# Where the gathered-row steps stand in VectorE's queue: pinned by an estimate of when their row lands, with a finer estimate of each instruction

## Chip, cores and metric

One core of a Trainium2 chip. The metric is the device time of one launch in microseconds; the time before is 3278.47 us, the median of three runs (3274.97 to 3279.72).

## What is computed

One residual block on 1024 tokens of width 1024, in f32. The last of its three parts is PEER: each token picks 16 of 16384 single-neuron experts for each of 8 heads.

```
x = x + hybrid_mixer(rmsnorm(x))         # gated DeltaNet (4 heads) | RG-LRU, one projection in, one out
x = x + cross_attention(rmsnorm(x), rmsnorm(mem))
x = x + peer_ffn(rmsnorm(x))
out = rmsnorm(x)

def peer_ffn(h):
    q = (t @ wq)                         # 8 heads x 2 halves of 128
    s1, i1 = top_k(q1 @ subkeys1, 16);  s2, i2 = top_k(q2 @ subkeys2, 16)
    best, pos = top_k(s1[:, None] + s2[None, :], 16)
    idx = i1[pos // 16] * 128 + i2[pos % 16];  gate = softmax(best)
    act = gelu(einsum('phkd,pd->phk', u_tab[idx], t)) * gate
    return einsum('phk,phkd->pd', act, v_tab[idx])
```

## The kernel before

**Stages.** The mixer works through four chunks of 256 tokens (tiles qkv, cy, lxf, W, gd, go); attention and the choice of experts follow it in units of 128, 128, 256, 256 and 256 tokens (X, hT, sc, s, i, cand, best, pos, e). For tokens 256 to 767 the experts are done densely: a gate stage turns the chosen indices into a gate matrix (one-hot rows oh from iot and keys, scaled on ScalarE into ohg, multiplied on TensorE into gd, copied into stage and written out), and a dense stage then runs 128 blocks of 128 experts (`hidden` and `out`: dh, dg, dah, dal, po; 48 matmuls of 512 columns per block). For the other four blocks of 128 tokens each expert row is gathered: GpSimd issues one indirect DMA of 128 rows of 4 KB (`fetch`, L1134), and VectorE does one **row step** on it (`step`): 512 steps take the dot product with u (rb, hdot), 512 add a row of v scaled by ga. So there are 1024 row steps, of which every one is a scalar_tensor_tensor over 128x1024; six row buffers (NROW) turn over, five gathers run ahead.

**What sets the order.** The kernel is traced as Python; streams (`together`) hand over pieces by an estimate of the time. Class `Engine` keeps it: every traced instruction goes through `f`, and `spend` adds a fixed part and a rate per element to the engine's clock `at` and remembers when each tile is ready (`known`). `Paced.tick` does so for TensorE, and whenever its clock has advanced by `pace` it traces a row step (before the dense stage only if VectorE's clock is less than SLACK ahead and the oldest row is estimated to have landed, `late_row`). `moved` estimates when a transfer lands. In the dense stage (`pe.real` off) the pace counts TensorE's work alone.

The framework then schedules the trace: each engine takes its instructions by trace order as they become ready in the framework's own reckoning, so an instruction whose input is not ready is overtaken by later ones. A row step is exempt: `tc.keep_in_program_order` puts it behind everything that VectorE was given before it in the trace. On the chip each engine runs its own queue strictly in that final order.

All VectorE and ScalarE instructions carry L82 (the helper's call), matmuls L106, transposes L111, the gathers L1134; so rows are told apart by tiles.

Of the kernel before, what the change touches and what calls it, by code (L numbers as in the profile page):

```python
# [8 lines left out]
F = mybir.dt.float32  # L9
BF = mybir.dt.bfloat16  # L10
# [3 lines left out]
AF = mybir.ActivationFunctionType  # L14
OP = mybir.AluOpType
# [3 lines left out]
S = 1024  # L19
# [4 lines left out]
TD = 2 * T  # L24
# [11 lines left out]
RANK = (1, 1, 1, 0)  # L36
HOP, SLACK, WAIT = 100.0, 8000.0, 1000.0
SHARE = (6.0, 1.0, 6.0, 1.0)
L_NORM, L_STEP, L_CONV, L_SOFT, L_GATE = 14000.0, 2500.0, 4000.0, 6000.0, 1500.0
PACES = (2800.0, 2800.0, 2800.0, 3500.0)  # L40
PACE_G, PACE_D = 3500.0, 2250.0
FIRST = 0
EARLY = T
UNITS = ((0, 1), (128, 1), (256, 2), (512, 2), (768, 2))
# [5 lines left out]
def block_kernel(ctx: ExitStack, tc: tile.TileContext, a):  # L50
# [21 lines left out]
    class Engine:  # L72

        def __init__(self, engine, fixed, rate):
            self.engine, self.fixed, self.rate = engine, fixed, rate
            self.at = self.total = self.end = 0.0

        def __getattr__(self, op):
            call = getattr(self.engine, op)

            def f(*args, **kw):
                r = call(*args, **kw)  # L82
                aps = [x for x in list(args) + list(kw.values()) if isinstance(x, bass.AP)]
                if op == "dma_start":
                    moved(prod(args[0].shape) * 4)
                else:
                    self.spend(aps)
                return r
            return f

        def spend(self, aps, n=0):
            t0 = max([self.at] + [known(x) for x in aps[1:]])
            ns = self.fixed + self.rate * (n or max(prod(x.shape[1:]) for x in aps))
            self.at = t0 + ns
            self.end = max(self.end, self.at)
            self.total += ns
            wrote(aps[0], self.at + HOP)

    class Paced(Engine):
# [5 lines left out]
        def matmul(self, out, l, r, **kw):  # L105
            self.engine.matmul(out, l, r, **kw)  # L106
            self.rate = 1.67 if r.dtype == F else 0.42
            self.tick([out, l, r])

        def transpose(self, out, i, ident):  # L110
            self.engine.transpose(out, i, ident)  # L111
            self.rate = 0.43
            self.tick([out, i])
# [10 lines left out]
    sp = Engine(nc.sync, 0.0, 0.0)  # L124
    act, dve = Engine(nc.scalar, 200.0, 0.72), Engine(nc.vector, 68.0, 1.04)

# [978 lines left out]

    todo, fetched = [], []
    blocks = {}
# [31 lines left out]
    def late_row():  # L1139
        return bool(fetched) and fetched[0][4] > max(dve.at, pe.at) + WAIT  # L1140

    def step():
        while todo and len(fetched) < NROW - 1:
            fetch()
        if not fetched:
            return False
        row, ph, k, t, _ = fetched.pop(0)
        B = blocks[row]
        if ph == "u":
            if k == 0:  # L1150
                dve.scalar_tensor_tensor(B["h"], B["h"], B["rs"], B["w"], op0=OP.mult, op1=OP.mult)
                B["hd"] = gat.tile([128, 128], F, name="hdot", bufs=1)
            tc.keep_in_program_order(
                dve.scalar_tensor_tensor(t, t, 1.0, B["h"], op0=OP.mult, op1=OP.mult,
                                         accum_out=B["hd"][:, k:k + 1]))
            if k == 120:
# [6 lines left out]
        else:  # L1163
            tc.keep_in_program_order(
                dve.scalar_tensor_tensor(B["x"], t, B["a"][:, k:k + 1], B["x"], op0=OP.mult, op1=OP.add))
            if k == 127:
# [98 lines left out]
    with tc.tile_pool(name="dn", bufs=1, side="right") as d2, \  # L1265
            tc.tile_pool(name="dps", bufs=1, space=bass.MemoryType.PSUM) as dps:
        pe.pace, pe.real = PACE_D, False
        dense(dn[0], d2, dps, hT, raws)
# [66 lines left out]
```

## Time and profile before

| | |
|---|---|
| median of three runs | 3278.47 us |
| the profiled execution's own time | 3275.43 us |
| its span | 3273.7 us |
| TensorE (PE) busy | 2987.4 us, 91% |
| VectorE (DVE) busy | 2737.6 us, 84% |
| ScalarE (ACT) busy | 1277.8 us, 39% |
| GpSimd (POOL) busy | 1431.4 us, 44% |
| moved by DMA | 941.66 MB, mean 288 GB/s |

The busy times are sums over the whole span. The stages have different limits, so the sections below read the trace by stretches, which are bounded by events found in VectorE's timeline: the first convolution cy of the second, third and fourth mixer chunk (392, 712, 1055 us), the first one-hot row of the gate stage (1353 us), the first matmul of the dense stage (1790 us), and TensorE's last instruction (3255 us).

### The profile page before, as it was taken

The numbers are of one execution on the slowest core, as the hardware profiler recorded it, in microseconds if no ns is written. First come the engines' busy times: TensorE is split into PE (matmuls) and PEld (weight loads), VectorE is DVE, ScalarE is ACT, GpSimd is POOL, SyncE is SP. The second block draws the span as 40 slices with busy tenths as digits, with TensorE's granted clock in tenths as the row PEclk, the third lists the DMA queues.
The fourth block names the chain that finished last, engine by engine and source line by source line (L and its number), as shares of the span: only waits on it lengthen the run. The fifth ranks groups of instructions, "written<-read, shape, count | busy, mean of one in ns | idle before, by whom it ended". The sixth has DMA issues, their size and how long they took to land.

```text
span 3273.7 us, 46519 instructions
## 1 busy us (share of the span) xinstructions
PE 2987.4 (91%) x16212; PEld 2559.6 (78%) x16212; DVE 2737.6 (84%) x5999; ACT 1277.8 (39%) x2694; POOL 1431.4 (44%) x1046
## 2 busy tenths in 40 slices
PE   6999997699999989898857899999999999999998
PEld 6888887678988878887746677888888878888886
DVE  7634776877787898898999798888999989899998
ACT  6843363236322642376357332222222222222222
POOL 0000233334433344243345375556666655566663
PEclk9999998899999999998968899999999999999999
DMA  5346788688888769888888799999999899999995
GB/s 170 110 143 208 248 281 308 232 285 284 308 292 291 251 223 332 301 281 302 303 289 273 267 329 334 333 340 330 344 333 328 319 334 333 330 341 327 339 331 198
DMA packets 321547, 941.66 MB, mean 288 GB/s; under 512 B 28912, under 2 KB 108832, under 8 KB 319264
## 3 DMA queue, kind: packets, MB, share of 16 engines
q0 software_dynamic: 148048, 538.04, 46.8%
q1 hardware_dynamic: 107216, 367.08, 30.9%
q10 hardware_dynamic: 66048, 33.56, 3.7%
q8 instruction: 128, 2.10, 0.3%
q14 instruction: 107, 0.88, 0.1%
HBM read 894.53 MB, written 44.04 MB: 287 GB/s over the span
## 4 chain that ended last, share of the span: by engine, by line
PE 61%; DVE 20%; DMA 9%; ACT 5%; issue 3%; POOL 1%; SPq 0%; ACTq 0%; DVEq 0%; POOLq 0%
PE dh L106 21%; PE po L106 20%; PE pj L106 15%; DVE rb L82 6%; DMA rb<-in_u,idx 4%; PE gd L106 3%; DVE oh L82 3%; DMA gd<-stage 2%; DMA w<-in_pwq 1%; PE tp L111 1%; PE sc L106 1%; DVE cy L82 1%; ACT ohg L82 1%; DVE i L82 1%; ACT L82 1%
## 5 line engine op out<-in xcount | busy, mean ns | idle before, releaser
L1134 POOL DMA_INDIRECT rb<-in_u,idx x512 | 677.4, 1323 | 1111.9 <-DVE rb L82 497.0
L1134 POOL DMA_INDIRECT rb<-in_v,idx x512 | 745.0, 1455 | 690.3 <-DVE rb L82 478.7
L82 DVE SCALAR_TENSOR_TENSOR rb<-rb 128x1024 f32<-128x1024 f32 x512 | 613.1, 1218 | 90.2 <-DMA rb<-in_u,idx 90.2
L82 DVE SCALAR_TENSOR_TENSOR rb<-rb,ga 128x1024 f32<-128x1024 f32 x512 | 655.0, 1279 | 11.2 <-DMA rb<-in_v,idx 4.9
L106 PE MATMUL pj<-hT,w 128*128 128x256 f32 (+1 forms) x2880 | 590.6, 358 | 16.2 <-DMA w<-in_pwq 11.8
L106 PEld LDWEIGHTS pj<-hT,w 128*128 128x128 f32 x2880 | 491.8, 195 | 73.5 <-DMA w<-in_pwq 13.1
L106 PE MATMUL dh<-hT_h,uh 128*128 128x512 f32 x1024 | 407.1, 398 | 21.4 <-ACT dg L82 20.7
L106 PE MATMUL po<-vh,dah 128*128 128x512 f32 x1024 | 404.8, 395 | 9.7 <-DVE acc L82 8.7
L106 PE MATMUL dh<-hT_l,uh 128*128 128x512 f32 x1024 | 406.2, 397 | 0.0
L106 PE MATMUL dh<-hT_h,ul 128*128 128x512 f32 x1024 | 406.1, 397 | 0.0
L106 PE MATMUL po<-vh,dal 128*128 128x512 f32 x1024 | 405.2, 396 | 0.4 <-DVE dal L82 0.4
L106 PE MATMUL po<-vl,dah 128*128 128x512 f32 x1024 | 405.3, 396 | 0.0
L82 ACT CAST uh<-ur 128x1024 fp32r<-128x1024 f32 x128 | 134.7, 1052 | 561.0 <-PE dh L106 352.8
L106 PE MATMUL gd<-ohg,oh 128*128 128x128 f32 x1024 | 183.7, 332 | 81.4 <-ACT ohg L82 54.5
L106 PEld LDWEIGHTS dh<-hT_h,uh 128*128 128x128 f32 x1024 | 193.2, 189 | 69.3 <-ACT dg L82 21.6
L106 PEld LDWEIGHTS gd<-ohg,oh 128*128 128x128 f32 x1024 | 163.8, 228 | 101.9 <-ACT ohg L82 80.5
L106 PEld LDWEIGHTS po<-vh,dah 128*128 128x128 f32 x1024 | 192.3, 188 | 58.4 <-DVE acc L82 10.0
L106 PEld LDWEIGHTS dh<-hT_h,ul 128*128 128x128 f32 x1024 | 193.0, 189 | 47.0
L106 PEld LDWEIGHTS dh<-hT_l,uh 128*128 128x128 f32 x1024 | 193.2, 189 | 46.4
L106 PEld LDWEIGHTS po<-vl,dah 128*128 128x128 f32 x1024 | 192.3, 188 | 47.2
L106 PEld LDWEIGHTS po<-vh,dal 128*128 128x128 f32 x1024 | 192.3, 188 | 47.1 <-DVE dal L82 0.8
L82 DVE TENSOR_TENSOR ul<-ur,uh 128x1024 fp32r<-128x1024 f32 x128 | 156.0, 1222 | 48.7 <-ACT uh L82 27.6
(339 smaller groups left out, 4757.4 us busy)
## 6 DMA issues: line engine op xcount, KB each, us to landing
ur<-in_ut SPq DMA_DIRECT2D x128, 512.0 KB
vr<-in_v SPq DMA_DIRECT2D x128, 512.0 KB
w<-in_wA SPq DMA_DIRECT2D x80, 512.0 KB
w<-in_pwq SPq DMA_DIRECT2D x80, 512.0 KB
gd<-stage ACTq DMA_DIRECT2D x32, 1024.0 KB
G<-gd SPq DMA_DIRECT2D x16, 2048.0 KB
w<-in_wout SPq DMA_DIRECT2D x40, 512.0 KB
w<-in_wq SPq DMA_DIRECT2D x40, 512.0 KB
```

Of the source, the lines that this page charges most:

```text
L82: r = call(*args, **kw)
L106: self.engine.matmul(out, l, r, **kw)
L111: self.engine.transpose(out, i, ident)
L1134: pool.indirect_dma_start(out=t, out_offset=None, in_=a[ph], in_offset=bass.IndirectOffsetOnAxis(ap=B["idx"][:, k:k + 1], axis=0))
```

## The change

1. A row step is no longer held behind everything traced. `behind` looks through a log of VectorE's traced instructions with their estimated ends, takes the last one that is estimated to be over by the time the row lands plus WAIT (1 us), and ties the step behind that one and behind the step before it (an order alone, no semaphore).
2. The estimate goes by form of instruction: `form` adds a fixed part for an accumulated output, for a per-partition scale on ScalarE, for a table load there, for a scalar_tensor_tensor, a max_index and a match_replace on VectorE; it doubles the scan and halves bf16. The constants of all three engines rise or change (VectorE's fixed part from 68 to 150 ns).
3. The paces change with it: 2800 to 3200 (in the estimate's ns of TensorE), 3500 to 4000, and in the dense stage from a fixed 2250 to DENSE over the steps that are left, so that these are spread over the whole of it.

```diff
-HOP, SLACK, WAIT = 100.0, 8000.0, 1000.0
+HOP, SLACK, WAIT = 130.0, 8000.0, 1000.0
-PACES = (2800.0, 2800.0, 2800.0, 3500.0)
-PACE_G, PACE_D = 3500.0, 2250.0
+PACES = (3200.0, 3200.0, 3200.0, 4000.0)
+PACE_G, DENSE = 4000.0, 1441000.0
+TABLES = {AF.Exp: (0,), AF.Tanh: (0, 1), AF.Gelu_apprx_tanh: (1,), AF.Sqrt: (2,)}
...
-                    self.spend(aps)
+                    self.spend(aps, *self.form(op, args, kw, aps))
+                    self.log.append((r.ins, self.at))
...
+        def form(self, op, args, kw, aps):
+            n = max(prod(x.shape[1:]) for x in aps)
+            more = 0.0
+            if self is act:
+                if isinstance(kw.get("scale"), bass.AP):
+                    more += 130.0
+                if "accum_out" in kw:
+                    more += 200.0
+                tables = TABLES.get(args[2]) if len(args) > 2 else None
+                if tables and self.table not in tables:
+                    self.table = tables[0]
+                    more += 1280.0
+            else:
+                if op == "scalar_tensor_tensor":
+                    more += 60.0
+                if "accum_out" in kw or op in ("max_index", "match_replace"):
+                    more += 80.0
+                if op == "tensor_tensor_scan":
+                    n *= 2
+                elif n > 64 and all(x.dtype == BF for x in aps):
+                    n //= 2
+            return n, more
...
-            self.rate = 1.67 if r.dtype == F else 0.42
+            self.rate = 1.7 if r.dtype == F else 0.46
...
-            self.rate = 0.43
+            self.rate = 0.85
...
-    act, dve = Engine(nc.scalar, 200.0, 0.72), Engine(nc.vector, 68.0, 1.04)
+    act, dve = Engine(nc.scalar, 165.0, 0.83), Engine(nc.vector, 150.0, 1.04)
...
+    def behind(r, land):
+        past = [i for i, t in dve.log[:-1] if t <= land + WAIT][-1:] + steps[-1:]
+        for i in past:
+            tc.add_manual_dep(r.ins, i.name, mybir.DependencyInfo(
+                mybir.DependencyClass.NoSync, mybir.DependencyReason.DATA), reason="rows")
+        steps.append(r.ins)
+        del dve.log[:-200]
...
-        row, ph, k, t, _ = fetched.pop(0)
+        row, ph, k, t, land = fetched.pop(0)
+        stepped[0] += 1
...
-            tc.keep_in_program_order(
-                dve.scalar_tensor_tensor(t, t, 1.0, B["h"], op0=OP.mult, op1=OP.mult,
-                                         accum_out=B["hd"][:, k:k + 1]))
+            behind(dve.scalar_tensor_tensor(t, t, 1.0, B["h"], op0=OP.mult, op1=OP.mult,
+                                            accum_out=B["hd"][:, k:k + 1]), land)
...
-            tc.keep_in_program_order(
-                dve.scalar_tensor_tensor(B["x"], t, B["a"][:, k:k + 1], B["x"], op0=OP.mult, op1=OP.add))
+            behind(dve.scalar_tensor_tensor(B["x"], t, B["a"][:, k:k + 1], B["x"],
+                                            op0=OP.mult, op1=OP.add), land)
...
-        pe.pace, pe.real = PACE_D, False
+        pe.pace, pe.real = DENSE / (2.0 * (S - TD) - stepped[0]), False
```

What the finished programs hold is the same in kind and number, but for one instruction of ScalarE's (a table load); the order differs on every engine before the dense stage. Counted in VectorE's queue, by the stretches named above (bounds by the same instructions in both programs; 32 MAX_INDEX on pos are the choice of experts for two blocks of 128 tokens, its first level is MAX_INDEX on i):

| stretch of VectorE's queue | row steps before, after | MAX_INDEX on pos | MAX_INDEX on i | oh<-oh |
|---|---|---|---|---|
| second chunk (392 to 712 us) | 98, 112 | 16, 16 | 32, 32 | 25, 25 |
| third chunk (712 to 1055 us) | 117, 115 | 0, 32 | 60, 64 | 0, 15 |
| fourth chunk (1055 to 1353 us) | 99, 135 | 32, 32 | 48, 64 | 40, 45 |
| gate stage, first to last one-hot row (1353 to 1790 us) | 127, 116 | 64, 32 | 84, 64 | 40, 20 |
| after it | 583, 546 | 0, 0 | 0, 0 | 40, 40 |

Two places in VectorE's queue show it. First the end of the fourth chunk's recurrence, whose products W (masks wm, levels 5 and 6) TensorE waits for. Before, six steps stand in one run behind the level's W, and the next unit's first-level choice (s, i) follows:

```order
L82 SCALAR_TENSOR_TENSOR n_y<-n_t,n_y 128x2
L82 TENSOR_TENSOR W<-gd,wm_85 128x512
L82 COPY rs_512_11047<-n_y 128x2
L82 TENSOR_TENSOR oh<-oh,ib 128x1024
L82 TENSOR_TENSOR oh<-oh 128x64x8
L82 TENSOR_TENSOR oh<-oh 128x64x4
L82 TENSOR_TENSOR oh<-oh 128x64x2
L82 TENSOR_TENSOR e_384_11079<-oh 128x64
L82 SCALAR_TENSOR_TENSOR rb,hdot<-rb 128x1024 x6
L82 MAX s_0_11125<-sc 128x8
L82 MAX_INDEX i_0_11127<-s_0_11125,sc 128x8
```

The same place in the changed program:

```order
L84 MATCH_REPLACE mr_11708<-best,cand 128x80
L84 SCALAR_TENSOR_TENSOR rb,hdot<-rb 128x1024
L84 TENSOR_TENSOR W<-gd,wm_85 128x512
L84 MAX best<-mr_11708 128x8
L84 SCALAR_TENSOR_TENSOR rb,hdot<-rb 128x1024
L84 MAX_INDEX pos<-best,mr_11708 128x8
L84 SCALAR_TENSOR_TENSOR rb,hdot<-rb 128x1024 x2
L84 MAX best<-cand 128x8
L84 TENSOR_TENSOR W<-gd,wm_86 128x512
L84 MAX_INDEX pos<-best,cand 128x8
L84 MATCH_REPLACE mr_11733<-best,cand 128x80
```

The steps now stand singly between the small instructions of a choice (best, pos) that came in the gate stage before, and up to two of them directly ahead of a W.

Second the dense stage, one pair of expert blocks. Before, nine steps stand from one pair's first ul to the last vl, four or three of them in a run:

```order
L82 TENSOR_TENSOR dal<-dg,dah 128x512
L82 SCALAR_TENSOR_TENSOR rb<-rb,ga 128x1024 x4
L82 TENSOR_TENSOR ul<-ur,uh 128x1024
L82 TENSOR_TENSOR dg<-dg,G 128x512
L82 TENSOR_TENSOR acc<-acc,po_20072 128x512
L82 TENSOR_TENSOR dal<-dg,dah 128x512
L82 SCALAR_TENSOR_TENSOR rb<-rb,ga 128x1024 x3
L82 TENSOR_TENSOR acc<-acc,po_20102 128x512
L82 TENSOR_TENSOR vl<-vr,vh 128x1024
L82 SCALAR_TENSOR_TENSOR rb<-rb,ga 128x1024
```

The like rows of the changed program:

```order
L84 TENSOR_TENSOR dal<-dg,dah 128x512
L84 SCALAR_TENSOR_TENSOR rb<-rb,ga 128x1024 x4
L84 TENSOR_TENSOR ul<-ur,uh 128x1024
L84 TENSOR_TENSOR dg<-dg,G 128x512
L84 TENSOR_TENSOR acc<-acc,po_19170 128x512
L84 SCALAR_TENSOR_TENSOR rb<-rb,ga 128x1024
L84 TENSOR_TENSOR dal<-dg,dah 128x512
L84 SCALAR_TENSOR_TENSOR rb<-rb,ga 128x1024 x2
L84 TENSOR_TENSOR acc<-acc,po_19200 128x512
L84 TENSOR_TENSOR vl<-vr,vh 128x1024 x2
L84 SCALAR_TENSOR_TENSOR rb<-rb,ga 128x1024
```

One of the three steps that followed dal now stands ahead of it, and the second vl is no longer parted from the first by a step. TensorE's queue in the dense stage is the same in both programs.

## Rows read from the trace of the kernel before

**Rows 1.** Busy time by stretch, all engines (stretch, its us, busy us and instructions by engine):

```profile
core 0: us, PE busy (x) PEld busy (x) DVE busy (x) ACT busy (x) POOL busy (x), PEclk, DMA share, GB/s
392.00:712.00 320.00, 266.32 (x1731) 242.50 (x1730) 244.57 (x755) 118.89 (x301) 116.75 (x102) 0.89 0.79 274
...
712.00:1055.00 343.00, 322.98 (x2018) 289.50 (x2018) 269.63 (x708) 131.09 (x328) 134.19 (x117) 0.99 0.84 294
...
1055.00:1353.00 298.00, 272.61 (x1776) 247.76 (x1776) 255.66 (x837) 122.26 (x295) 113.00 (x95) 0.98 0.78 274
...
1353.00:1790.00 437.00, 343.04 (x1944) 305.17 (x1944) 404.88 (x1251) 279.79 (x770) 168.04 (x129) 0.86 0.88 290
...
1738.00:1790.00 52.00, 41.73 (x232) 35.46 (x231) 48.93 (x80) 49.57 (x144) 26.21 (x16) 0.93 0.92 276
...
1857.00:3255.00 1398.00, 1387.99 (x5938) 1114.92 (x5937) 1272.52 (x1511) 397.68 (x505) 859.91 (x560) 1.00 0.90 327
```

**Rows 2.** Waits of PE, 392 to 712 us (who waited for whom: us, times, longest):

```profile
PE tp L111 <- DVE go L82: 11.6, 1, 11.6
...
PE gd L106 <- DVE best L82: 6.5, 3, 4.4
```

**Rows 3.** Groups of DVE instructions, 1055 to 1353 us (busy us, mean ns, idle before):

```profile
L82 DVE SCALAR_TENSOR_TENSOR rb<-rb 128x1024 f32<-128x1024 f32 x58 | 69.5, 1216 | 10.1 <-DMA rb<-in_u,idx 10.1
...
L82 DVE SCALAR_TENSOR_TENSOR rb<-rb,ga 128x1024 f32<-128x1024 f32 x35 | 44.6, 1275 | 0.2
```

**Rows 4.** DMA totals, 1055 to 1353 us (q0: packets, MB, share of 16 engines):

```profile
DMA packets 24616, 81.74 MB, mean 274 GB/s; under 512 B 2604, under 2 KB 5164, under 8 KB 24591
...
q0 software_dynamic: 13383, 48.73, 47.1%
```

**Rows 5.** Waits of PE, 1353 to 1790 us:

```profile
PE gd L106 <- ACT ohg L82: 54.5, 51, 5.3
...
PE gd L106 <- DVE oh L82: 15.5, 5, 6.2
```

**Rows 6.** Groups of DVE instructions, 1353 to 1790 us:

```profile
L82 DVE FIND_INDEX8 i<-s,sc 128x8 uint32<-128x128 f32 x42 | 11.8, 281 | 0.0
...
L82 DVE FIND_INDEX8 i<-s,mr 128x8 uint32<-128x128 f32 x42 | 11.6, 276 | 0.0
...
L82 DVE MATCH_REPLACE8 mr<-s,sc 128x128 f32<-128x128 f32 x42 | 11.4, 272 | 0.0
...
L82 DVE MAX8 s<-sc 128x8 f32<-128x128 f32 x42 | 11.4, 279 | 0.0
...
L82 DVE MAX8 s<-mr 128x8 f32<-128x128 f32 x42 | 11.4, 271 | 0.0
...
L82 DVE FIND_INDEX8 pos<-best,mr 128x8 uint32<-128x80 f32 x32 | 7.4, 231 | 0.0
...
L82 DVE FIND_INDEX8 pos<-best,cand 128x8 uint32<-128x80 f32 x32 | 7.4, 231 | 0.0
...
L82 DVE MAX8 best<-mr 128x8 f32<-128x80 f32 x32 | 7.3, 229 | 0.1
...
L82 DVE MATCH_REPLACE8 mr<-best,cand 128x80 f32<-128x80 f32 x32 | 7.1, 223 | 0.0
...
L82 DVE MAX8 best<-cand 128x8 f32<-128x80 f32 x32 | 7.0, 229 | 0.0
...
L82 DVE TENSOR_TENSOR oh<-oh 128x512 bf16<-128x512 bf16 (+2 forms) x24 | 7.8, 323 | 0.2
...
L82 DVE TENSOR_TENSOR oh<-oh,ib 128x1024 bf16<-128x1024 bf16 x8 | 5.5, 684 | 0.1
...
L82 DVE TENSOR_TENSOR oh<-oh,iota 128x1024 bf16<-128x1024 bf16 x8 | 5.4, 680 | 0.1
```

**Rows 7.** Waits of PE from 1790 us to the end:

```profile
PE dh L106 <- ACT dg L82: 20.7, 2, 17.9
...
PE po L106 <- DVE acc L82: 8.7, 3, 5.2
```

More of the change, by code (lines that the diff above doesn't have):

```diff
@@ L76, in __init__ @@
             self.at = self.total = self.end = 0.0
+            self.table, self.log = None, []
         def __getattr__(self, op):
@@ L86, in f, with spend @@
                 else:
-                    self.spend(aps)
-                return r
-            return f
-        def spend(self, aps, n=0):
+                    self.spend(aps, *self.form(op, args, kw, aps))
+                    self.log.append((r.ins, self.at))
+                return r
+            return f
+        def form(self, op, args, kw, aps):
[20 more added lines that the diff above has]
+            return n, more
+        def spend(self, aps, n=0, more=0.0):
             t0 = max([self.at] + [known(x) for x in aps[1:]])
-            ns = self.fixed + self.rate * (n or max(prod(x.shape[1:]) for x in aps))
+            ns = self.fixed + more + self.rate * (n or max(prod(x.shape[1:]) for x in aps))
             self.at = t0 + ns
@@ L1101, in dense @@
         finish(acc, row3, xs[0][:, NT - 1, :])
-    todo, fetched = [], []
+    todo, fetched, stepped = [], [], [0]
     blocks = {}
@@ L1140, in late_row @@
         return bool(fetched) and fetched[0][4] > max(dve.at, pe.at) + WAIT
+    def behind(r, land):
[5 more added lines that the diff above has]
+        del dve.log[:-200]
+    steps = []
     def step():
```

## The prediction, made before the changed kernel ran

> **What bounds the kernel now.** I read the busy times by stretch first [rows 1]. They show three regimes. From 1857 to 3255 us TensorE is busy for 1387.99 of 1398 us: the dense stage runs at TensorE's own pace, and VectorE, at 1272.52 us, fits beside it. So nothing done for VectorE there can give back more than TensorE's idle time. From 1353 to 1790 us, the gate stage (G), VectorE is busy for 404.88 of 437 us (93%) and TensorE for 343.04: VectorE is the bound, but for the last 52 us, where ScalarE is busy for 49.57. The waits of TensorE agree: 54.5 us for ohg, which waits for oh, and 15.5 us for oh itself [rows 5]. The three mixer chunks before it (A to 712, B to 1055, C to 1353 us) are mixed: TensorE is busy 83%, 94% and 91%, VectorE 76%, 79% and 86%. In A part of what TensorE lacks comes from VectorE's order: 11.6 us for go and 6.5 us for best [rows 2].
>
> **The change part by part.** No instruction of VectorE's is added, so its total work stays; the question is in which stretch it stands, which the counts in the two programs say, and how well it fills the gaps.
>
> *Row steps.* One takes 1216 or 1275 ns in C [rows 3], say 1.25 us. A gets 14 more (+17.5 us of VectorE's time), B two fewer (-2.5), C 36 more (+45), G 11 fewer (-14), the rest 37 fewer (-46). Each takes its gather along: C gets 36 more on GpSimd, which was busy there for 113.00 us with 95 instructions [rows 1], 1.19 us each, so about 156 of some 300 us; that queue holds little else. SyncE's loads for a block of rows stay as many. The pin is an order and no semaphore, so no new wait is issued; what it changes is who stands behind whom. A step whose row is late now holds back VectorE instructions that were traced before it, where it used to hold back only later ones.
>
> *The choice of experts.* With the new estimate the streams hand over in another order. In G 32 of 64 MAX_INDEX on pos, 20 of 84 on i and 20 of 40 oh<-oh go. By the rows of G [rows 6]: half of the five pos and best groups (36.2 us) is 18.1 us, 20/84 of the five i and s groups (57.6 us) is 13.7 us, half of the three oh groups (18.7 us) is 9.4 us; 41 us, and I add nothing for the small rest. The same 32 on pos turn up in B, with 15 oh<-oh and 4 on i (18.1 + 7.0 + 2.7 = 28 us); C gets 16 on i and 5 oh<-oh (11.0 + 2.3 = 13 us).
>
> So VectorE's work becomes: A 244.57 + 17.5 = 262 us, B 269.63 + 28 - 2.5 = 295, C 255.66 + 45 + 13 = 314, G 404.88 - 14 - 41 = 350, and some 46 less of the rest.
>
> *A (320 us).* 262 us of VectorE's work fit easily. At best the two waits of TensorE go (-18), at worst all the added work shows (+17.5). I take -3, since the steps now give way to a choice but also stand ahead of other things.
>
> *B (343 us).* 295 us is 86%, the share at which C runs now, while TensorE, 94% busy, sets the length. From -5 to +28 (all of what is added beyond the steps it loses); I take +5, near what VectorE's 73 idle us can hide.
>
> *C (298 us).* 314 us do not fit into 298. VectorE without any gap gives +16; with the 42 us of idle time that it has now, +58. Transfers bound it as well: 81.74 MB pass now, of which q0, the gathers, 48.73 [rows 4], for 93 steps [rows 3] 0.524 MB each. 135 steps make 70.7 MB, with the 33.0 of the rest 104 MB; at the 327 GB/s of the dense stage [rows 1] that is 317 us, +19. I take +30, which is VectorE at 96%: the single placement is made to fill gaps, but G, where VectorE is the bound, reaches 93% with what lies open to it.
>
> The Trainium skill, DMA: Bandwidth & Descriptors, Specifications, puts the limit of HBM per core at about 358 GB/s; by it the 104 MB would take an estimated 290 us, less than the stretch has now, and transfers would be no bound in C. The dense stage's 327 GB/s is at a DMA share of 0.90 [rows 1], so the trace does not contradict that limit; the sum goes by the row, and by the page it would be the same, since VectorE's own time is the larger of the two.
>
> *G (437 us).* At its present 93%, 350 us of work take 378 us, -59; if TensorE took over at B's 94%, 343.04 us would take 365, -72. If only half of the 70 us that TensorE waits for ohg and oh go, -35: the last 52 us are ScalarE's and cannot shrink. I take -47, midway between -35 and -59.
>
> *Dense stage.* The steps per pair of blocks fall from about nine to about eight and a half. Of TensorE's idle time 20.7 us are a wait for dg, of which one of 17.9 us stays, at the stage's start; 8.7 us are for acc, which steps stand ahead of [rows 7]. From -9 to +3; I take -6. What follows 3255 us stays.
>
> **Sum.** -3 + 5 + 30 - 47 - 6 = -21 us against the profiled execution's 3275.43 us, so 3254. The median of the runs is 3.0 us above that execution, so **3257 us** against 3278.47. If all ends fell on one side the sum would run from -88 (-18 - 5 + 16 - 72 - 9) to +72 (17.5 + 28 + 58 - 35 + 3).
>
> **Rivals.**
>
> *Nothing net (3278 us).* C gives back what G gains, -40 against +40. For it: VectorE's work is the same to the instruction, and from 392 to 1790 us it is busy 1174.7 of 1398 us and gets another 46. Against it: there were 223 us idle to put them in.
>
> *C chokes (slower, 3299 us).* A step that stands ahead of earlier work stops VectorE until its row lands; in C that costs 10.1 us already [rows 3], and gathers come 1.45 times as often there. Then the 42 us of idle time stay, C costs +58 where I have +30, and TensorE, waiting more, is granted less clock: 0.98 in C now, 0.89 in A, where it waits more [rows 1]. Between its two levels of 1.2 and 2.4 GHz that step down costs 272.61 x (0.98 / 0.89 - 1) = 27.6 us of its work; half of it, 14 us, is what I price. 58 - 30 + 14 = 42 more than the forecast's sum: -21 + 42 = +21, with everything else as forecast, 3299. It decides from the point at which C takes over 45 us longer than now. For it: VectorE above 100% of the old length; against it: singly placed steps let the chain through more often than a run of six.
>
> The Trainium skill, Perfetto Trace Analysis, section Matmul Optimizations, says that TensorE scales its power with its use, so that matmuls should run back to back in batches; it speaks against a stretch that VectorE holds up. The trace agrees in kind: G, where TensorE waits most, is granted 0.86, the dense stage 1.00 [rows 1]. By it alone C would lose the whole 28 us.
>
> *All of it overlaps (3209 us).* A -8, B 0, C +16, G -68, dense stage -9: -69. For it: 223 us of idle time and a finer estimate that keeps choices from being piled up in front of go. Against it: C's floors.
>
> *The change not doing what it says:* the log keeps 200 instructions, and a step could find none early enough and be tied to the step before alone. The queues show otherwise (no runs longer than seven); under 2%, and it would look like the second rival.
>
> **How the numbers follow.** What a measurement can tell here is about 0.2%, 6.6 us, so faster is under 3272 and slower above 3285. The forecast (3225 to 3272) gets 0.45; no net change 0.15; C choking 0.25, spread from 3285 to 3325; full overlap 0.15, spread from 3190 to 3225. Faster is 0.45 + 0.15 = 0.60, same 0.15, slower 0.25. Below 3202 lies some 0.07 and above 3306 some 0.10, so the range is 3202 to 3306; the forecast's own is 3225 to 3272.
>
> **What would show it.** Right: in the busy times by stretch, bounded by the same instructions, C at 320 to 340 us with VectorE at 95% or more, G at 375 to 405 us, TensorE's waits for ohg and oh together at 25 to 45 us, the dense stage within 10 us of before with acc below 5 us. Wrong: C not longer (then the gaps took it all, and the third rival stands), C above 345 us with waits of rb for its gather above 25 us and a clock under 0.95 (second), or G hardly shorter (then ScalarE or TensorE bounds it, and the choice was beside it).

## The result: 0.9% slower, by the fourth chunk

The changed kernel takes 3303.75 us (median of 4 runs, 3302.12 to 3312.40), the kernel before 3276.72 us (4 runs, 3273.17 to 3279.72). The ratio is 1.0088, with an interval of 1.0067 to 1.0109. The forecast was 3257 us: the sign is wrong. The time lies inside the range of 3202 to 3306, near where the rival "C chokes" (3299) had put it. The profiled execution of the changed kernel took 3302.98 us, its span is 3301.2 us.

One correction comes first. The bounds that stand ahead for the second, third and fourth chunk (392, 712 and 1055 us) are wrong: I read them off rows of the timeline in which several cy rows are merged. By the first cy row of each chunk they are 356.0, 689.4 and 1029.3 us, so [rows 1] cut each of these stretches 23 to 36 us late. The starts of the gate stage and of the dense stage were right, and the counts of row steps went by instructions, so they stand. From here on A, B, C, G and the dense stage (with what follows it) are cut by the same instructions in every kernel.

The kernel before, busy time by stretch (columns as in [rows 1]):

```profile
356.00:689.40 333.40, 278.29 (x1816) 253.82 (x1815) 246.87 (x762) 125.08 (x317) 117.79 (x104) 0.90 0.78 274
689.40:1029.30 339.90, 319.44 (x2001) 285.95 (x2000) 267.80 (x716) 129.70 (x325) 136.46 (x118) 0.98 0.84 296
1029.30:1353.00 323.70, 298.31 (x1895) 270.24 (x1894) 278.50 (x892) 130.96 (x320) 118.97 (x101) 0.98 0.79 274
1353.00:1789.90 436.90, 342.94 (x1944) 305.07 (x1943) 404.78 (x1251) 279.69 (x770) 167.94 (x129) 0.86 0.88 290
1789.90:3273.70 1483.80, 1439.95 (x6144) 1155.74 (x6144) 1335.28 (x1635) 423.55 (x538) 882.67 (x577) 0.99 0.89 322
```

The changed kernel, the same five stretches (its lines have moved: L84 is the helper of VectorE and ScalarE, L133 the matmuls, L138 the transposes):

```profile
358.80:695.70 336.90, 273.92 (x1824) 250.16 (x1823) 258.97 (x792) 125.53 (x318) 141.73 (x117) 0.91 0.81 293
695.70:1042.80 347.10, 324.07 (x2015) 288.77 (x2014) 292.44 (x910) 138.00 (x337) 137.64 (x116) 0.98 0.82 290
1042.80:1420.70 377.90, 325.88 (x1968) 291.83 (x1966) 326.87 (x1047) 133.03 (x320) 163.65 (x137) 0.92 0.81 292
1420.70:1836.60 415.90, 322.71 (x1847) 290.58 (x1847) 356.81 (x915) 276.05 (x761) 168.50 (x119) 0.85 0.86 283
1836.60:3301.20 1464.60, 1437.39 (x6144) 1154.86 (x6144) 1285.25 (x1596) 419.49 (x535) 773.51 (x538) 0.99 0.87 312
```

Read the second number of each row. The first chunk, which ends at the first row, grew by 2.8 us, A by 3.5, B by 7.2 and C by 54.2; G fell by 21.0 and the dense stage by 19.2. The sum is +27.5, the difference of the two spans. So the whole loss, twice over, is in C. In C VectorE (the third busy time) went from 278.50 to 326.87 us, its share from 86.0% to 86.5%: it took on 48 us of work, and its idle time there did not shrink. TensorE's matmuls there rose from 1895 to 1968, its busy share fell from 92% to 86% and its clock from 0.98 to 0.92.

VectorE's waits in C, before and then after:

```profile
DVE rb L82 <- DMA rb<-in_u,idx: 10.1, 6, 3.3
DVE X L82 <- PE pj L106: 7.5, 6, 2.0
```

```profile
DVE X L84 <- PE pj L133: 19.1, 7, 4.0
DVE rb L84 <- DMA rb<-in_u,idx: 10.2, 13, 1.2
```

The waits for gathered rows of u are the same, 10.1 and 10.2 us; what grew is the wait for TensorE's projections. TensorE in turn waits in C for things that VectorE makes on the recurrence's chain. After the change:

```profile
PE tp L138 <- DVE go L84: 11.1, 1, 11.1
PE gd L133 <- DVE g L84: 6.9, 1, 6.9
PE tp L138 <- ACT oT L84: 5.4, 2, 5.1
PE pj L133 <- ACT lge L84: 4.4, 3, 1.9
```

Of these go had 2.4 us before. In G the forecast had TensorE's two waits on the one-hot rows fall from 70 to between 25 and 45 us. They stayed, 55.0 and 15.3 us against [rows 5]:

```profile
PE gd L133 <- ACT ohg L84: 55.0, 42, 10.4
PE gd L133 <- DVE oh L84: 15.3, 7, 3.9
```

From the dense stage's start TensorE's waits did fall, from [rows 7]:

```profile
PE dh L133 <- ACT dg L84: 12.1, 2, 11.4
PE po L133 <- DVE acc L84: 1.6, 1, 1.6
```

### The profile page after: what moved, and what is told of

The parts are those of the page before. It is cut to its first block, busy times and chain, and to the rows that moved or that the text cites. A ratio compares the mean times of both kernels' runs of the same rounds, so it can differ in the third digit from the quotient of the medians.

```text
span 3301.2 us, 46535 instructions
## 1 busy us (share of the span) xinstructions
PE 2994.6 (91%) x16212; PEld 2567.2 (78%) x16212; DVE 2724.2 (83%) x5999; ACT 1281.2 (39%) x2693; POOL 1392.6 (42%) x1046
## 4 chain that ended last, share of the span: by engine, by line
PE 66%; DVE 16%; DMA 9%; ACT 5%; issue 4%; POOL 1%; SPq 0%; ACTq 0%; DVEq 0%; POOLq 0%
PE dh L133 21%; PE po L133 21%; PE pj L133 17%; DVE rb L84 5%; PE gd L133 3%; DVE oh L84 2%; DMA gd<-stage 2%; PE sc L133 2%; DMA subk<-in_subk 2%; DMA rb<-in_u,idx 1%; PE tp L138 1%; DMA w<-in_wA 1%; ACT ohg L84 1%; DMA w<-in_pwq 1%; ACT L84 1%
## 5 line engine op out<-in xcount | busy, mean ns | idle before, releaser
L1161 POOL DMA_INDIRECT rb<-in_v,idx x512 | 707.2, 1381 | 793.9 <-DVE rb L84 511.7
L84 DVE SCALAR_TENSOR_TENSOR rb<-rb,ga 128x1024 f32<-128x1024 f32 x512 | 655.6, 1280 | 13.4 <-DMA rb<-in_v,idx 8.0
L84 DVE SCALAR_TENSOR_TENSOR rb<-rb 128x1024 f32<-128x1024 f32 x512 | 612.3, 1220 | 21.1 <-DMA rb<-in_u,idx 21.0
L133 PE MATMUL pj<-hT,w 128*128 128x256 f32 (+1 forms) x2880 | 587.6, 358 | 17.5 <-DMA w<-in_pwq 10.5
L133 PEld LDWEIGHTS pj<-hT,w 128*128 128x128 f32 x2880 | 493.6, 194 | 77.1 <-DMA w<-in_pwq 11.5
L133 PE MATMUL dh<-hT_h,uh 128*128 128x512 f32 x1024 | 406.8, 397 | 12.8 <-ACT dg L84 12.1
L133 PE MATMUL dh<-hT_l,uh 128*128 128x512 f32 x1024 | 406.2, 397 | 0.0
L133 PE MATMUL dh<-hT_h,ul 128*128 128x512 f32 x1024 | 406.1, 397 | 0.0
L133 PE MATMUL po<-vh,dah 128*128 128x512 f32 x1024 | 404.0, 394 | 1.6 <-DVE acc L84 1.6
L133 PE MATMUL po<-vl,dah 128*128 128x512 f32 x1024 | 404.9, 395 | 0.0
L133 PE MATMUL po<-vh,dal 128*128 128x512 f32 x1024 | 404.3, 395 | 0.0
L84 ACT CAST uh<-ur 128x1024 fp32r<-128x1024 f32 x128 | 134.6, 1052 | 593.0 <-PE dh L133 339.1
L84 DVE TENSOR_TENSOR ul<-ur,uh 128x1024 fp32r<-128x1024 f32 x128 | 156.6, 1224 | 115.6 <-ACT uh L84 72.5
L133 PE MATMUL gd<-ohg,oh 128*128 128x128 f32 x1024 | 180.6, 333 | 75.6 <-ACT ohg L84 55.0
L133 PEld LDWEIGHTS dh<-hT_h,uh 128*128 128x128 f32 x1024 | 193.0, 188 | 60.8 <-ACT dg L84 13.0
L133 PEld LDWEIGHTS gd<-ohg,oh 128*128 128x128 f32 x1024 | 163.5, 231 | 92.2 <-ACT ohg L84 84.6
L133 PEld LDWEIGHTS po<-vh,dah 128*128 128x128 f32 x1024 | 191.9, 187 | 49.1 <-DVE acc L84 2.1
L133 PEld LDWEIGHTS dh<-hT_h,ul 128*128 128x128 f32 x1024 | 193.0, 188 | 47.0
L133 PEld LDWEIGHTS dh<-hT_l,uh 128*128 128x128 f32 x1024 | 193.1, 189 | 46.5
L133 PEld LDWEIGHTS po<-vl,dah 128*128 128x128 f32 x1024 | 192.1, 188 | 47.3
L133 PEld LDWEIGHTS po<-vh,dal 128*128 128x128 f32 x1024 | 192.1, 188 | 46.1
```

Of the source, the lines that this page charges most:

```text
L1161: pool.indirect_dma_start(out=t, out_offset=None, in_=a[ph], in_offset=bass.IndirectOffsetOnAxis(ap=B["idx"][:, k:k + 1], axis=0))
```

## The experiments

The change has three parts (pin, estimate, paces). The theory that these rows suggest: the pin helps, and the 36 more row steps in C cost more than G and the dense stage return. The rivals: the pin itself hurts, since freer steps stand ahead of their rows; the estimate's order of the streams hurts, whatever the loads. All ratios below are to the kernel before, run on the same chip beside them. The runs used four chips, on which the kernel before had medians of 3282 to 3286 us. Where a profiled execution lies over 5 us from the median of its runs, that is said. The stretches of the kernel before are from its first profile (3275 us), so on these chips it runs some 7 to 10 us longer, and differences of a few us between stretches say little: spread_alone, whose stretches up to the dense one are ordered as before, has A, B, C and G at 333.6, 336.2, 325.1 and 443.7 us, up to 7 us off the first profile.

### The parts one at a time

**pin_alone**: the kernel before with the new pin only.

```diff
-            tc.keep_in_program_order(
-                dve.scalar_tensor_tensor(...))
+            behind(dve.scalar_tensor_tensor(...), land)
```

> The kernel before with the new pin alone: old estimate, old paces. VectorE's queue keeps its counts by stretch (98, 117, 99, 127 row steps and 583 after became 97, 121, 98, 127 and 581). If the loss comes from where single steps stand (ahead of instructions that TensorE waits for), this alone is slower: 3287 us or more against 3277. If it comes from the 36 more steps in the fourth chunk, or from the new order that the estimate makes of the streams, this run is within 8 us of before, and the fourth chunk stays at 315 to 335 us.

Measured: 3269.45 us, ratio 0.9941 (0.9921 to 0.9961). A, B and C:

```profile
357.90:675.20 317.30, 269.83 (x1816) 246.27 (x1815) 244.26 (x766) 124.74 (x317) 118.45 (x103) 0.91 0.82 288
675.20:1004.60 329.40, 316.06 (x1997) 283.61 (x1996) 264.87 (x700) 127.41 (x322) 146.89 (x121) 0.99 0.86 309
1004.60:1336.20 331.60, 300.98 (x1899) 271.78 (x1898) 276.09 (x909) 133.98 (x321) 112.89 (x100) 0.96 0.77 266
```

A is 16.1 us shorter than before and B 10.5, with nearly the same steps in them (97 for 98 and 121 for 117). C is 7.9 longer and the dense stage 11.2. The pin alone makes this kernel faster by 0.6%. In A the gain has a cause in view: VectorE's wait for rows of u, before and then with the pin, fell by as much as the stretch.

```profile
DVE rb L82 <- DMA rb<-in_u,idx: 19.7, 10, 3.6
```

```profile
DVE rb L83 <- DMA rb<-in_u,idx: 3.7, 2, 2.3
```

**old_pin**: the changed kernel with the old pin.

```diff
     def behind(r, land):
-        past = [i for i, t in dve.log[:-1] if t <= land + WAIT][-1:] + steps[-1:]
-        for i in past:
...
+        tc.keep_in_program_order(r)
         steps.append(r.ins)
```

> The changed kernel with the old pin (each step behind all of VectorE's work traced before it): new estimate and new paces stay, so the steps by stretch stay (112, 118, 132, 116, 546). If the pin is the loss: 3285 us or less. If load or estimate is: 3296 to 3312, the fourth chunk again 365 us or more. If the new pin is worth something in itself, this run is slower than the changed kernel's 3304.

Measured: 3379.71 us, ratio 1.0284 (1.0264 to 1.0303). C, and VectorE's first wait in it:

```profile
1082.50:1490.50 408.00, 328.66 (x1950) 293.99 (x1948) 331.51 (x1065) 132.98 (x319) 161.39 (x136) 0.90 0.76 267
```

```profile
DVE rb L84 <- DMA rb<-in_u,idx: 34.3, 21, 5.3
```

With the old pin VectorE waits 34.3 us in C for rows of u, with the new one 10.2. So the new pin is not what made the kernel slow; without it the loss would be three times as large.

**spread_alone**: the kernel before with the dense stage's pace spread over the steps that are left.

```diff
-        pe.pace, pe.real = PACE_D, False
+        pe.pace, pe.real = 1321205.0 / (2.0 * (S - TD) - stepped[0]), False
```

> The kernel before with its dense stage's steps spread evenly over what is left (the old fixed pace replaced by the estimated total of the stage over the steps left); the front is the same program. Only TensorE's waits for acc (8.7 us in the profile of before) and the idle time at the end of the steps can move: 3268 to 3277 us by every theory. If it is 3260 or less, the dense stage's gain of 19 us in the changed kernel comes from the spread and not from fewer steps in it.

Measured: 3284.29 us, ratio 1.0001 (0.9980 to 1.0022). Its dense stage takes 1483.0 us, before 1483.8. The spread is worth nothing by itself.

### The loads

**fewer1**: the changed kernel with fewer steps in C (88 in place of 135, 587 in place of 546 after G).

```diff
-PACES = (3200.0, 3200.0, 3200.0, 4000.0)
+PACES = (3200.0, 3200.0, 3200.0, 5400.0)
```

> The changed kernel with the fourth chunk's pace raised from 4000 to 5400: 88 row steps in that chunk where the changed kernel has 135 (before: 99), 122 in the gate stage, 587 after it. If the load of the fourth chunk is the loss, that chunk falls from 378 us to 325 to 340, the gate stage and the dense stage stay within 10 us of the changed kernel's and before's, and the whole is 3255 to 3285 us. If the order that the new estimate makes of the streams is the loss whatever the load, it stays at 3292 or more.

Measured: 3282.15 us, ratio 0.9989 (0.9976 to 1.0003), as the load theory had it. The profiled execution is the fastest, 21 us under the median, so its stretches serve for large differences only. C and the dense stage:

```profile
1039.30:1375.50 336.20, 310.75 (x1969) 281.82 (x1967) 268.62 (x923) 131.50 (x318) 98.91 (x90) 0.98 0.73 253
...
1789.40:3259.50 1470.10, 1439.60 (x6144) 1154.20 (x6144) 1332.84 (x1637) 424.94 (x538) 872.13 (x577) 0.99 0.89 325
```

This splits C's 54.2 us. With as many matmuls as in the changed kernel (1969 and 1968) but 47 steps fewer, C is 41.7 us shorter, 0.89 us for a step; 15.1 of these are TensorE's own work, 325.88 against 310.75 us, at a clock of 0.92 and 0.98. The other 12.5 us remain against before, though C has 11 steps fewer than there; its 74 more matmuls, moved here with the choice of experts, make TensorE busy for 12.4 us more. With fewer steps TensorE is busy for 92% of C again, as before.

**even**: the changed kernel with about as many steps per stretch as before, in the changed order of the choice.

```diff
-PACES = (3200.0, 3200.0, 3200.0, 4000.0)
+PACES = (3200.0, 3600.0, 3200.0, 5000.0)
```

> The changed kernel (its pin, its estimate, its spread) with paces that put about as many row steps into each stretch as before: 98, 112, 95, 124 and 595 of them in the second, third and fourth chunk, the gate stage and after it (before: 98, 117, 99, 127, 583; changed: 112, 115, 135, 116, 546). The choice of experts keeps the changed order. Load theory (the chunks are as long as the steps put into them make them): the second and third chunk fall to the 317 and 329 us that the pin alone gave, the fourth to 330 to 340, gate stage 414, dense stage and tail 1470 to 1480: some 3235 in all, 0.983 to 0.989 of before. Rival (the new estimate's order of the streams itself lengthens the chunks): second and third chunk stay at 333 to 348, the total comes out at 0.996 to 1.000 of before, as with fewer steps in the fourth chunk alone.

Measured: 3250.26 us, ratio 0.9900 (0.9879 to 0.9921), the profiled execution 7 us below it. Its stretches:

```profile
357.80:679.30 321.50, 268.59 (x1819) 244.63 (x1818) 242.39 (x763) 124.83 (x318) 122.87 (x104) 0.93 0.80 285
679.30:1026.80 347.50, 324.75 (x2020) 290.57 (x2019) 289.82 (x920) 138.90 (x337) 133.18 (x112) 0.98 0.80 285
1026.80:1359.70 332.90, 310.59 (x1969) 281.90 (x1967) 276.09 (x933) 132.01 (x319) 107.84 (x96) 0.99 0.76 266
1359.70:1769.80 410.10, 321.49 (x1848) 289.30 (x1848) 364.78 (x996) 273.77 (x761) 176.25 (x129) 0.86 0.92 303
1769.80:3241.50 1471.70, 1440.84 (x6144) 1154.92 (x6144) 1342.06 (x1645) 423.91 (x538) 903.22 (x585) 0.99 0.90 327
```

A is at 321.5 us with 98 steps, 15.4 us less than with 112; C at 332.9 with 95, 45.0 us less than with 135. B did not fall to 329 but stayed at 347.5: it has only 3 steps fewer than in the changed kernel, and it still holds the 32 MAX_INDEX on pos and their matmuls. The ratio lies between what the two theories gave, nearer the load theory. From 1.0088 to 0.9900 is 1.9%, so the loads alone turn a change that is worth 1% into one that costs 0.9%.

**even_old_pin**: the same loads and estimate, with the old pin.

```diff
-PACES = (3200.0, 3200.0, 3200.0, 4000.0)
+PACES = (3200.0, 3600.0, 3200.0, 5000.0)
...
-        past = [i for i, t in dve.log[:-1] if t <= land + WAIT][-1:] + steps[-1:]
-        for i in past:
...
+        tc.keep_in_program_order(r)
         steps.append(r.ins)
```

> The same paces and estimate, but each step pinned behind all that was traced, as before: 96, 117, 97, 119 and 595 steps. If the new pin is worth more the more steps a chunk holds, it is worth here about what it was worth in the kernel before, 0.6%: this run comes out 0.4 to 0.8% above the run with the new pin. Rival (the new estimate traces steps so that the old pin hurts more, whatever their number): 1.5 to 2.5% above, as in the changed kernel, with every chunk 20 us or more longer.

Measured: 3324.06 us, ratio 1.0120 (1.0094 to 1.0145), 2.3% above the run with the new pin. My expectation fell, its rival held (though A, at some 337 us, is 15 us longer and not 20): under the new estimate the old pin costs some 2% at even loads (1.0120 against 0.9900) as at the changed ones (1.0284 against 1.0088). Waits in C, of VectorE and of TensorE:

```profile
DVE rb L84 <- DMA rb<-in_u,idx: 28.5, 12, 7.9
```

```profile
PE tp L138 <- DVE best L84: 14.1, 1, 14.1
PE gd L133 <- DVE n_t L84: 9.1, 1, 9.1
```

With the new pin the wait for u rows in C is 0.5 us. Why the old one costs more under this estimate than in the kernel before (0.6%) was not tried further.

**no_form3**: the changed kernel without the estimate by form, with even loads (101, 108, 96, 130, 589). The second level of the choice of experts then falls back to the order before; of its first level C keeps the 64 MAX_INDEX on i of the changed kernel (48 before).

```diff
-                    self.spend(aps, *self.form(op, args, kw, aps))
+                    self.spend(aps)
...
-    act, dve = Engine(nc.scalar, 165.0, 0.83), Engine(nc.vector, 150.0, 1.04)
+    act, dve = Engine(nc.scalar, 200.0, 0.72), Engine(nc.vector, 68.0, 1.04)
...
-PACES = (3200.0, 3200.0, 3200.0, 4000.0)
-PACE_G, DENSE = 4000.0, 1441000.0
+PACES = (3200.0, 2850.0, 3100.0, 3800.0)
+PACE_G, DENSE = 3600.0, 1441000.0
```

> The changed kernel without the estimate by form (VectorE's and ScalarE's old constants, TensorE's new rates, the new pin, the spread dense stage), with paces that put 101, 108, 96, 130 and 589 row steps into the five stretches: nearly those of the run with even loads. The choice of experts then stands as before (none of the 32 MAX_INDEX on pos in the third chunk, 64 in the gate stage). If the estimate by form, by moving the choice ahead, is worth the 0.4% between even loads and the pin alone: this comes out at 0.993 to 0.996 of before, third chunk 325 to 333 us, gate stage 435 to 442. Rival (what helped was TensorE's new rates or the spread): 0.988 to 0.991, as with even loads.

Measured: 3263.78 us, ratio 0.9936 (0.9916 to 0.9956), the profiled execution 8 us above it. The ratio is as forecast for "the form, by moving the choice, is worth 0.4%", though the interval reaches into that of even loads. The stretches do not bear out the reason. B, C, G and the dense stage:

```profile
688.60:999.20 310.60, 297.95 (x1906) 268.31 (x1905) 242.96 (x627) 127.80 (x318) 125.27 (x109) 0.99 0.85 299
999.20:1341.90 342.70, 321.50 (x2005) 292.01 (x2005) 282.80 (x952) 135.13 (x327) 110.53 (x100) 0.98 0.78 269
1341.90:1773.20 431.30, 338.10 (x1912) 300.91 (x1910) 406.77 (x1261) 280.66 (x767) 169.84 (x132) 0.86 0.89 292
1773.20:3269.70 1496.50, 1449.72 (x6144) 1160.83 (x6144) 1339.53 (x1642) 424.78 (x539) 882.46 (x583) 0.99 0.89 322
```

With even loads G is 21.2 us shorter than here and C 9.8, but B is 36.9 longer: A, B, C and G together take 1412.0 us there and 1412.8 here. So the moved choice gives nothing net where it moves. The difference of the two profiles lies in the dense stage, 1471.7 against 1496.5 us with about the same steps. Some of that may be the executions, which lie 7 us below and 8 us above their medians; the cause of the rest is open.

Counted in the program, the form is also where the extra steps come from: with the changed paces but without it the stretches hold 85, 108, 93, 103 and 635 steps; with it 112, 115, 135, 116 and 546. TensorE's clock in the estimate counts its waits for VectorE, and before the dense stage the pace counts that clock; so where the estimate makes VectorE slower, TensorE's clock runs longer and hands VectorE more steps.

### Where the pin stands

**even_late** (first diff) and **even_early** (second): even loads, with the pin behind what is over 4 us after the row lands, or 2 us before it, in place of 1 us after.

```diff
-        past = [i for i, t in dve.log[:-1] if t <= land + WAIT][-1:] + steps[-1:]
+        past = [i for i, t in dve.log[:-1] if t <= land + 4000.0][-1:] + steps[-1:]
```

```diff
-        past = [i for i, t in dve.log[:-1] if t <= land + WAIT][-1:] + steps[-1:]
+        past = [i for i, t in dve.log[:-1] if t <= land - 2000.0][-1:] + steps[-1:]
```

> The run with even loads, but a step is pinned behind the last VectorE instruction that is estimated to be over 4 us after its row lands, in place of 1 us; loads the same (97, 113, 94, 125, 595). If the place of the pin is sensitive (the old pin, behind everything traced, cost 2.2%), 3 us more cost a part of it, here a third: 0.996 to 1.000 of before, with the chunks 5 to 10 us longer each. Rival (only steps traced far ahead of their neighbours matter): within 0.2% of even loads, 0.988 to 0.992.

> The run with even loads, but a step is pinned behind the last VectorE instruction that is estimated to be over 2 us before its row lands; loads the same (99, 113, 94, 123, 595). If a freer step stands ahead of its row and stops VectorE (the reason on record for a slow fourth chunk), VectorE's waits of rb for its gather, 14.5 us in the gate stage with even loads, grow to 25 us or more in the chunks and the gate stage, and it comes out at 0.993 to 1.000 of before. Rival (rows land long before their step, five gathers ahead): waits of rb unchanged within 5 us a stretch, 0.986 to 0.991.

Measured: late 3292.63 us, ratio 1.0031 (1.0016 to 1.0046); early 3265.08 us, ratio 0.9944 (0.9929 to 0.9959), its profiled execution 12 us above that. Late costs 1.3% against even loads, more than expected: A, B and C are 10.1, 5.0 and 5.8 us longer, and the dense stage, with the same 595 steps, 34.0. There TensorE waits

```profile
PE dh L133 <- ACT dg L84: 17.0, 2, 14.2
PE po L133 <- DVE acc L84: 24.5, 11, 3.5
```

against 5.4 and 8.7 us with even loads. Early costs 0.4%, but not in the way I gave: VectorE's waits for gathered rows are 0.3, 0.4, 4.9 and 5.4 us in A, B, C and G, 11.0 in all against 16.4 with even loads (0, 1.4, 0.5 and 14.5). A step that stands ahead of its row is thus not what stops VectorE here. One microsecond is the best of three places; that it is best for its reason is not shown. Most of what late costs is in the dense stage, and runs with about as many steps there, in slightly other orders, scatter by nearly as much (1470 to 1497 us).

### The gate stage

**gate_half**: the changed kernel with 52 steps in G and 610 after it.

```diff
-PACE_G, DENSE = 4000.0, 1441000.0
+PACE_G, DENSE = 8000.0, 1441000.0
```

> The changed kernel with half of the gate stage's row steps sent on to the dense stage (52 in place of 116 in the gate stage, 610 in place of 546 after it). 64 steps of 1.25 us are 80 us of VectorE's 356.8 there. Hand-over theory (the gate stage is set by the chain from VectorE's one-hot rows through ScalarE's scaling to TensorE): the stage stays at 400 to 416 us, TensorE's waits for ohg and oh stay at 60 to 75 us, VectorE's idle time there rises from 59 to above 115. Rival (VectorE's load still sets it): the stage falls to 335 to 365 us and the two waits to under 45. The dense stage, where VectorE has 1285 of 1465 us to do, takes 80 more: 0 to 15 us longer. Total against before: 1.007 to 1.013 by the first, 0.985 to 0.996 by the second.

Measured: 3268.08 us, ratio 0.9942 (0.9922 to 0.9962), the profiled execution 7 us above it. G, and TensorE's two waits in it:

```profile
1431.40:1784.50 353.10, 306.69 (x1848) 276.53 (x1848) 281.95 (x847) 269.95 (x757) 70.60 (x54) 0.92 0.77 234
```

```profile
PE gd L133 <- ACT ohg L84: 33.5, 51, 4.3
...
PE gd L133 <- DVE oh L84: 2.4, 2, 2.1
```

The hand-over theory, which I had formed from the unchanged 70 us, fell: G gave back 62.8 us for 74.9 us less of VectorE's work. Of the 62.8, 16 are TensorE's own work, at a clock of 0.92 in place of 0.85 (306.69 against 322.71 us).

**even_g1**: even loads, and 89 steps in G in place of 124, 630 after it.

```diff
-PACE_G, DENSE = 4000.0, 1441000.0
+PACE_G, DENSE = 5400.0, 1441000.0
```

> The run with even loads, but 35 row steps fewer in the gate stage (89 in place of 124) and 35 more after it (630 in place of 595). With half of the gate stage's steps sent on, that stage gave back 63 us for 64 steps and the dense stage took 24. If the dense stage takes the steps at that price: gate stage 373 to 382, dense stage 1480 to 1490, total 0.983 to 0.988 of before. Rival (above some 600 steps VectorE is full in the dense stage, 1342 us and 44 more of 1472, and TensorE waits for acc): dense stage 1500 to 1515, total 0.990 to 0.995.

Measured: 3217.45 us, ratio 0.9797 (0.9764 to 0.9830): faster than both kernels, and than either theory gave. G and the dense stage, and TensorE's wait in the latter:

```profile
1363.80:1728.40 364.60, 308.33 (x1847) 276.86 (x1847) 318.60 (x954) 270.12 (x758) 107.35 (x90) 0.91 0.88 281
1728.40:3219.00 1490.60, 1449.53 (x6144) 1159.23 (x6144) 1391.15 (x1688) 427.12 (x541) 952.62 (x624) 0.99 0.92 338
```

```profile
PE po L133 <- DVE acc L84: 20.5, 12, 3.9
```

G is 45.5 us shorter for 35 steps, the dense stage 18.9 us longer. TensorE's two waits in G, with even loads and then here:

```profile
PE gd L133 <- ACT ohg L84: 47.7, 40, 4.8
PE gd L133 <- DVE oh L84: 15.7, 8, 5.6
```

```profile
PE gd L133 <- ACT ohg L84: 38.3, 53, 4.1
...
PE gd L133 <- DVE oh L84: 4.6, 3, 3.8
```

**before_gate**: the kernel before, old pin and old estimate, with only its gate stage relieved (82 steps for 127) and the dense stage spread.

```diff
-PACE_G, PACE_D = 3500.0, 2250.0
+PACE_G, PACE_D = 4800.0, 2250.0
...
-        pe.pace, pe.real = PACE_D, False
+        pe.pace, pe.real = 1321205.0 / (2.0 * (S - TD) - stepped[0]), False
```

> The kernel before (old pin, old estimate, its order of the choice of experts) with only this changed: the gate stage traces 82 row steps in place of 127, and the dense stage spreads the 628 that are left. If the gate stage's row steps cost what they take on VectorE whatever the pin and the estimate (35 fewer gave 45 us back with even loads): gate stage 380 to 395 us in place of 437, dense stage 15 to 25 us longer, total 0.988 to 0.994 of before, so that some half of what the best run has is the load alone. Rival (the gate stage gives time back only in the changed order, where its choice of experts has been done earlier): gate stage above 415 us, total 1.000 to 1.006 of before.

Measured: 3259.39 us, ratio 0.9916 (0.9883 to 0.9949).

```profile
1349.80:1742.20 392.40, 326.20 (x1946) 293.07 (x1944) 351.25 (x1201) 277.58 (x767) 98.47 (x84) 0.90 0.83 260
1742.20:3256.80 1514.60, 1457.39 (x6144) 1159.70 (x6144) 1389.40 (x1684) 424.01 (x539) 948.98 (x621) 0.98 0.91 332
```

G is 44.5 us shorter for 45 steps, the dense stage 30.8 us longer (more than the 15 to 25 expected). The load in G is worth its 0.8% without the pin and the new estimate (the spread, which this run has, is worth nothing by itself), and the remaining 1.2% of the best run come on top with the pin and the new order.

## Why the prediction was wrong, step by step

The forecast's sum was -21 us and the profiles give +27.5. Two terms carry the miss about equally, C by 24 us and G by 26; the dense stage makes up for 13 of it. Both terms fail at the same step: how much of VectorE's time a stretch fills, 96% in C and 93% in G by the forecast, 86% in each as measured.

**C (+30 forecast, +54.2 measured): the step that failed.** The forecast had the singly placed steps fill VectorE's gaps: "VectorE at 96%". VectorE's added work was sized near enough, 48 us against 58, but VectorE ended 86.5% busy, and a step put into C lengthened it by most of its own time. From fewer1 to the changed kernel VectorE has 58.3 us more to do and C is 41.7 longer; from even loads it is 45.0 for 50.8. So 11 to 28% of the added work went into gaps, where the forecast put 28 of 58 us. My upper bound, +58, was the better number: the 42 us of idle time in the row of C had a cause that the change does not touch, and full use of it had no row to stand on. I argued from G, a stage of another kind.

That VectorE's share is 86% before and after is no rule. It is 80% in fewer1 and 83% with even loads. There TensorE's share is the one that stays, 92% and 93%, against 92% before. I read it so: with 88 to 99 steps C is as long as TensorE's work makes it, with 135 VectorE's queue sets it (TensorE 86% busy). This is argued from the shares and was not tried by itself.

**The matmuls that move with the choice: left out.** I moved VectorE's part of the choice from stretch to stretch, and none of TensorE's. C took 73 matmuls more, G had 97 fewer. In C that is 12.4 us of TensorE's time (fewer1), in a stretch where it is 92% busy before; it matches the 12.5 us that C keeps when the steps are taken out.

**G (-47 forecast, -21.0 measured): the same step.** VectorE's work was right, 356.8 us against 350, but its share fell from 93% to 86%, so I mis-sized the return: it lies outside even my smallest bound of -35, which had half of TensorE's 70 us of waits for ohg and oh go, and they stayed. The runs show two prices. Row steps taken out of G give back 0.83 to 0.99 us for each us of VectorE's (gate_half 62.8 for 74.9; before_gate 44.5 for 53.5; even_g1 45.5 for 46.2). The choice of experts taken out gives back half: 21.2 us for 42.0 (even loads against no_form3, with 6 steps fewer), 21.0 for 48.0 (the change itself, with 11 fewer). Two profiles of the same order differ by 7 us in G (436.9 and, in spread_alone, 443.7), so these prices are rough. That the choice had partly been filling VectorE's gaps, and left them open when it went, is the reading I would give; it was not tried by itself.

**Dense stage (-6 forecast, -19.2 measured).** The wait for dg fell from 20.7 to 12.1 us and that for acc from 8.7 to 1.6. My bound of -9 was too tight: it held the longest dg wait (17.9 us) to be fixed, which became 11.4, and even so the two terms that I named give 2.8 + 8.7 = 11.5. The reason was wrong as well. I put the gain down to 37 steps fewer, but in fewer1 the stage, with 587 steps against 583 before, is already 13.7 us shorter than before, and the changed kernel, with 41 fewer than that, is only 5.5 us shorter still. The rest is not settled: the spread gives 0.8 us by itself, the pin alone makes the stage 11.2 us longer, and with 581 to 595 steps it takes 1470 to 1506 us in nine runs. So no single price of a step can be read off the pairs (23.9 us for 64 in gate_half, 18.9 for 35 in even_g1, 30.8 for 45 in before_gate).

**A and B (-3 and +5 forecast, +3.5 and +7.2 measured).** The sizes are near by a cancellation: in A the pin returns 16.1 us (pin_alone) and 14 more steps take 15.4 (even loads); in B the pin returns 10.5, and the choice that came, with 9 steps fewer, takes 18 (347.5 with even loads against 329.4 in pin_alone).

**The rivals.** "C chokes" gave 3299 and its place, its length (above 45 us) and its clock (priced at 14 us; 15.1 by fewer1) hold. Its reason does not: waits for rows did not grow, the steps merely filled VectorE's queue. So the right rival had the wrong mechanism, and its test ("waits of rb above 25 us") would have cleared it. That its 3299 us came so near is in part luck: it had C at +72 (58 and 14 for the clock) and G at -47, and they came out at +54.2 and -21.0. The Trainium skill, Perfetto Trace Analysis, section Matmul Optimizations, has TensorE's power follow its use; C agrees, with a granted clock of 0.98 before and 0.92 after as TensorE's busy share fell from 92% to 86%. The transfer floor that I worked out for C, 317 us, bounds nothing at 377.9, and the 327 GB/s under it is no ceiling: the dense stage of even_g1 moved 338 GB/s, and C before moved 372 GB/s from 1269.3 to 1289.3 us. The latter is also above the limit that the prediction took the trace not to contradict.

**The change does what it says.** The pin is worth 0.6% by itself and some 2% under the new estimate. What made the whole slower is that the paces, in the units of the new estimate, put 36 more steps into the fourth chunk.

## What to carry to other kernels

When work moves into a stretch, price it at most of its own length, and let gaps take more only where a row shows which wait it would fill: in C each us of VectorE's added work cost 0.72 to 0.89 us. When work moves out, ask which work: in G steps gave back 0.83 to 0.99 us for each us, the choice of experts about half. Pricing each stretch at its present busy share would not have done it: that is right for C (+58) and as wrong for G (-59), and with the other terms of the forecast it comes to -5 us. Move the other engines' part of the work with it. When an estimate that drives a planner is refined, the paces and budgets in its units change meaning: set them again so that each stretch gets the load it had, and only then judge the rest. And a stretch that is slowed by one engine may be relieved more cheaply than it is reordered: moving 45 steps out of the gate stage of the kernel before gave 0.8%, where the whole change, at even loads, gave 1.0%.

## What was not expected of the hardware

In two stretches the waits of TensorE cost more than their length, since the granted clock was lower where it waited more. With as many matmuls, TensorE's own work was 325.88 us at a granted clock of 0.92 and 310.75 at 0.98 in the fourth chunk, 322.71 at 0.85 and 306.69 at 0.92 in the gate stage: 15 to 16 us in each, some 36% and a quarter of what relieving VectorE gave back there (41.7 and 62.8 us). This is also how 35 steps of 1.22 to 1.28 us, 46.2 us of VectorE's work, could return 45.5 us in the gate stage, though TensorE's waits for ohg and oh fell by only 20 us there (47.7 and 15.7 to 38.3 and 4.6): TensorE's own work fell by 13 us too, from 321.49 to 308.33, at 0.91 in place of 0.86. The 12 us that are left were not traced to a cause.
